# A pad of 64 bytes under the two parts of the gate and up weights

## The chip, the cores and the metric

The kernel runs on one core of a Trainium2 chip. Its metric is the device time of one execution in microseconds (us), lower is better. Before the change the median of three runs is 2303.36 us (2303.14 to 2303.79).

## The reference

One block of a streaming encoder on 512 positions of width 2048, all in float32: RMSNorm, one projection `W_in`, eight heads of a gated linear recurrence (HGRN2) and eight heads of forgetting attention (FoX), the output projection with a residual, then RMSNorm, a gated feed-forward part and a last RMSNorm. The change lies in the feed-forward part:

```python
def conv_ffn(h, w_gate, w_up, conv_w, conv_b, w_down):
    a = h @ w_gate
    a_pad = jnp.pad(a, ((0, 0), (CONV_WIDTH - 1, 0), (0, 0)))
    a = sum(conv_w[j] * a_pad[:, j:j + L] for j in range(CONV_WIDTH)) + conv_b
    return (jax.nn.silu(a) * (h @ w_up)) @ w_down
```

`w_gate` and `w_up` are 2048 x 5632, `w_down` is 5632 x 2048.

## The kernel before

Every large product is made of float32 values that are cut into two parts (hi and lo, type fp32r, one TensorE pass each), and three matmuls stand for one: hi by hi, hi by lo, lo by hi. ScalarE makes the hi part by a copy, VectorE the lo part by a subtraction.

The kernel has three stages. The first does the projections, the mixers and the output projection (lines up to 750). The second, the gate and up products, is the one that the change touches. The third does the down projection and the last norm.

The second stage goes through 44 units (`glu(f)`, lines 839 to 872), one for each 128 columns of `w_gate` and `w_up`. A unit is seven products (`product`, line 820) by Strassen's scheme on blocks of half the positions (256) and half the depth (1024). A product is eight blocks `j` of 128 columns, three matmuls each (lines 828, 829, 830), so the stage has 44 x 7 x 8 x 3 = 7392 matmuls. In each, the stationary operand is a 128 x 128 block of the weight tile `fhi` or `flo`, which TensorE loads anew for every matmul, and the moving operand is a 128 x 256 block of the activations (`b11h`, `b11l`, ... in the pools `tt` and `tl`).

The weights come from HBM into the pool `wf` (eight buffers `wq` of 4096 bytes a partition; `load`, line 769, by SyncE's queue, and with an addition on the way by GpSimd's, line 774). `prepare` (line 800) is called two products ahead (LEAD = 2): it adds where the scheme wants it (line 792), and cuts a `wq` into `fhi` (line 816, ScalarE) and `flo` (line 817, VectorE). These lie in the pool `wh`, LEAD + 2 = 4 buffers each of 4096 bytes, 32 KB a partition together. Above it lies the pool `gt` with the temporaries of a unit (`p1`, `u2`, `u3`, `a`, `uu`, `t`, `ah`, `al`); `ah` and `al` are stored to `actd` in HBM by SyncE's queue (line 872).

The order of the work is the program's: engines take their instructions in order and wait for each other by semaphores, which the framework derives from the tiles. A tile that is laid over the bytes of older, closed tiles waits for the last users of all of them. On each side of the memory pools stand one on the other, and a pool that is opened later starts where the last one ends.

Addresses: with the pads `even_sm`, `even` and `even_cm` the pools' sizes add up so that in the kernel before every tile of these pools starts at a multiple of 512 bytes within its partition: `wq` at 43520, `fhi` at 76288, `flo` at 92672, `gt` at 109056, the activations of `tl` at 27136 and of `tt` at 125440. A weight block of 128 float32 columns is 512 bytes, so each block of `fhi` and `flo` starts at such a multiple too. Tiles of the small pools don't: `onesd` (stationary operand of line 473) starts 96 bytes past a multiple of 512, `R2` (line 860) 160 bytes, `sq` (line 237) 416 bytes, and the gate weights `wf` of line 576 are blocks of 40 columns, 160 bytes each, which start 0, 160, 320, 480, 128, 288, 448 and 96 bytes past one.

Of the kernel before, what the change touches and what calls it, by code (L numbers as in the profile page):

```python
# [8 lines left out]
F32 = mybir.dt.float32  # L9
# [6 lines left out]
P = 128  # L16
# [23 lines left out]
FORM = KP * P  # L40
LEAD = 2
DMA_SUMS = True
EVEN = 376
EVEN_CM = 24
EVEN_SM = 40
# [11 lines left out]
def tile_hymba_block(ctx: ExitStack, tc: tile.TileContext, xT, wst, wgu, wdn, wfb, consts, out, out_t):  # L57
# [5 lines left out]
    def opened(name, bufs, side="left", **kw):  # L63
        cm = tc.tile_pool(name=name, bufs=bufs, side=side, reuse_waits="tile", **kw)
        pools[name] = (cm, cm.__enter__())
        return pools[name][1]

    def closed(*names):
        for name in names:
            pools.pop(name)[0].__exit__(None, None, None)  # L70
# [12 lines left out]
    even = opened("even", 1, "right")  # L83
    even.tile([P, EVEN], F32, name="even")
    cm = opened("cm", 1, "right")
# [606 lines left out]
    tt = opened("tt", 1, "right")  # L692
# [55 lines left out]
    tl = opened("tl", 1)  # L748
# [10 lines left out]


    wf = opened("wf", 8)
    wh = opened("wh", LEAD + 2)
    gt = opened("gt", 1)
    ORDER = ("a11", "s2", "a12", "s3", "s1", "a22", "s4")
# [5 lines left out]
    def load(f, name, q, q2=None):  # L770
        t = raw[f, name] = W()
        nc.sync.dma_start(out=t, in_=wgu[f, q])
        if q2 is not None:
            gp.dma_start(out=t, in_=wgu[f, q2], accum_op=ALU.add)  # L774

    def loads(f):

        if DMA_SUMS:
            load(f, "s1", 0, 1)
# [10 lines left out]
    def add(f, name, x, y, into=None):  # L790
        t = raw[f, name] = W() if into is None else into
        v.tensor_tensor(t, raw[f, x], raw[f, y], op=ALU.add)  # L792

    def sums(f):
        if not DMA_SUMS:
            add(f, "s1", "a21", "a22")
            add(f, "s3", "a21", "a11", raw[f, "a21"])
        add(f, "s2", "s1", "a11")
# [40 lines left out]
    def glu(f):  # L839
        cw = con[:, C_CW + 3 * f:C_CW + 3 * f + 3]  # L840
        g = 7 * f
        L, H = slice(0, QH), slice(QH, T)
        x, y, z, w = half(mm), half(mx), half(mm), half(mx)
        p1, u2, u3 = (G(n, (P, QH)) for n in ("p1", "u2", "u3"))
        a, uu = G("a"), G("uu")
        product(g, x)
        s.activation(p1, x, AF.Copy)
        product(g + 1, y)
        v.tensor_tensor(u2, p1, y, op=ALU.add)
        product(g + 2, x, first=False)  # L850
        s.activation(a[:, L], x, AF.Copy)
        product(g + 3, y, first=False)
        v.tensor_tensor(u3, p1, y, op=ALU.add)
        product(g + 4, z)
        v.tensor_tensor(uu[:, H], u3, z, op=ALU.add)
        product(g + 5, w)
        v.tensor_tensor(uu[:, L], u3, w, op=ALU.subtract)
        product(g + 6, z, first=False)
        v.tensor_tensor(a[:, H], u2, z, op=ALU.add)
        v.tensor_tensor(a, a, R2, op=ALU.mult)  # L860
        t = G("t")
        s.activation(t, a, AF.Identity, scale=cw[:, 2:3], bias=con[:, C_CB + f:C_CB + f + 1])
        v.scalar_tensor_tensor(t[:, 1:T], a[:, 0:T - 1], cw[:, 1:2], t[:, 1:T], op0=ALU.mult, op1=ALU.add)
        v.scalar_tensor_tensor(t[:, 2:T], a[:, 0:T - 2], cw[:, 0:1], t[:, 2:T], op0=ALU.mult, op1=ALU.add)
        v.tensor_tensor(uu, uu, nR2, op=ALU.mult)
        s.activation(t, t, AF.Silu)
        v.tensor_tensor(uu, uu, t, op=ALU.mult)
        hi, lo = G("ah", dt=F32R), G("al", dt=F32R)
        s.activation(hi, uu, AF.Copy)
        v.tensor_tensor(lo, uu, f32(hi), op=ALU.subtract)  # L870
        for i, part in enumerate((hi, lo)):
            nc.sync.dma_start(out=actd[f, i], in_=f32(part))
# [3 lines left out]
        prepare(g)  # L876
    for f in range(NF):
        glu(f)
    closed("gt", "wh", "wf", "tl", "tt")


    wr = opened("wr", 3)
# [189 lines left out]
```

## Time and profile before

| | us |
|---|---|
| median of the three runs | 2303.36 |
| the profiled execution | 2302.61 |
| its span, first to last instruction | 2300.9 |
| TensorE busy (matmul) | 2271.3 (99%) |
| VectorE busy | 1464.3 (64%) |
| ScalarE busy | 939.5 (41%) |
| granted TensorE clock, mean share | 0.995 |

The span is what the views divide; 1.7 us of the execution lie around it. A matmul's busy time holds its way through the array, so that neighbours overlap: what a stream of matmuls costs is read from the distance of their starts, not from the mean duration.

### The profile page before, as it was taken

What the parts mean: (1) busy time and instruction counts of PE and PEld (TensorE: products, weight loads), DVE (VectorE), ACT (ScalarE), POOL (GpSimd) and SP (SyncE); (2) the same over time, 40 slices, a digit from 0 to 9 for tenths busy, and PEclk for the clock granted to TensorE, in tenths of its full rate; (3) what the DMA queues carried; (4) which work ended last, traced back from release to release, by engine and by line L of the source; (5) the groups of instructions that cost most, each with busy time, mean ns of one, the idle gap of its engine ahead of it and who ended that gap; (6) DMA issues with size and microseconds to landing.
All of it is one profiled execution on the core that took longest, in us unless ns stands there. A gap on an engine that the chain in (4) does not pass through costs nothing. (4 is left out here: it accounts for less than half of the span.)

```text
span 2300.9 us, 34411 instructions
## 1 busy us (share of the span) xinstructions
PE 2271.3 (99%) x13662; PEld 2023.0 (88%) x13662; DVE 1464.3 (64%) x2194; ACT 939.5 (41%) x1484; POOL 172.0 (7%) x259
## 2 busy tenths in 40 slices
PE   8999999999999998999999999999999999999998
PEld 7888888788888887999999999999999788888886
DVE  6666467656457565888888888888888433333345
ACT  5333233334335444544444444444454222222234
POOL 4000000000000000000000000000000422000000
PEclk9999999999999999999999999999999999999999
DMA  5222222222222445877777778777776865323223
GB/s 176 84 83 83 96 77 93 75 87 76 90 83 74 142 161 170 227 205 216 209 207 211 200 207 219 213 207 209 212 197 171 316 261 194 101 96 101 92 95 116
DMA packets 112210, 352.67 MB, mean 153 GB/s; under 512 B 12816, under 2 KB 19088, under 8 KB 112048
## 3 DMA queue, kind: packets, MB, share of 16 engines
q1 hardware_dynamic: 89568, 272.67, 35.7%
q0 software_dynamic: 22336, 77.67, 15.2%
q8 instruction: 107, 1.75, 0.3%
q14 instruction: 55, 0.45, 0.1%
q10 hardware_dynamic: 144, 0.12, 0.0%
HBM read 318.96 MB, written 31.46 MB: 152 GB/s over the span
## 5 line engine op out<-in xcount | busy, mean ns | idle before, releaser
L159 DVE TENSOR_TENSOR wlo<-raw,whi 128x512 fp32r<-128x512 f32 x453 | 315.1, 697 | 456.3 <-ACT whi L158 415.9
L158 ACT ACTIVATE whi<-raw 128x512 fp32r<-128x512 f32 x453 | 285.0, 630 | 675.5 <-PE mxt L211 309.0
L816 ACT ACTIVATE fhi<-wq 128x1024 fp32r<-128x1024 f32 x308 | 326.4, 1060 | 375.9 <-PE pq L829 335.5
L817 DVE TENSOR_TENSOR flo<-wq,fhi 128x1024 fp32r<-128x1024 f32 x308 | 376.1, 1221 | 62.0 <-ACT fhi L816 59.0
L210 PE MATMUL mmt<-at,whi 128*128 128x512 f32 x896 | 354.8, 396 | 0.0
L212 PE MATMUL mmt<-at,wlo 128*128 128x512 f32 x896 | 349.7, 390 | 0.0
L211 PE MATMUL mmt<-at,whi 128*128 128x512 f32 x896 | 349.3, 390 | 0.0
L210 PE MATMUL mxt<-ot,whi 128*128 128x512 f32 x660 | 258.2, 393 | 3.5 <-ACT whi L158 2.7
L212 PE MATMUL mxt<-ot,wlo 128*128 128x512 f32 x660 | 257.4, 390 | 0.9 <-DVE wlo L159 0.9
L211 PE MATMUL mxt<-ot,whi 128*128 128x512 f32 x660 | 257.4, 390 | 0.3 <-DMA ot<-actd 0.3
L212 PEld LDWEIGHTS mmt<-at,wlo 128*128 128x128 f32 x896 | 168.2, 188 | 36.0
L210 PEld LDWEIGHTS mmt<-at,whi 128*128 128x128 f32 x896 | 168.3, 188 | 34.8 <-issue 2.0
L211 PEld LDWEIGHTS mmt<-at,whi 128*128 128x128 f32 x896 | 168.4, 188 | 33.1
L210 PEld LDWEIGHTS mxt<-ot,whi 128*128 128x128 f32 x660 | 124.2, 188 | 31.7 <-DMA ot<-actd 3.0
L211 PEld LDWEIGHTS mxt<-ot,whi 128*128 128x128 f32 x660 | 124.2, 188 | 27.4 <-DMA ot<-actd 1.6
L212 PEld LDWEIGHTS mxt<-ot,wlo 128*128 128x128 f32 x660 | 124.2, 188 | 26.7 <-DVE wlo L159 1.2
L774 POOL DMA_DIRECT2D wq<-wgu x88 | 75.9, 862 | 794.4 <-DVE flo L817 416.7
L792 DVE TENSOR_TENSOR wq<-wq 128x1024 f32<-128x1024 f32 x88 | 107.5, 1222 | 4.2 <-DMA wq<-wgu 2.7
L295 PE MATMUL mmt<-wlo,at 128*128 128x512 f32 x256 | 100.6, 394 | 4.9 <-DVE wlo L159 4.9
L828 PE MATMUL pq<-b11h,fhi 128*128 128x256 f32 x352 | 100.7, 286 | 3.6 <-ACT fhi L816 3.6
L293 PE MATMUL mmt<-whi,at 128*128 128x512 f32 x256 | 101.7, 397 | 1.6 <-ACT whi L158 1.6
L830 PE MATMUL pq<-b11h,flo 128*128 128x256 f32 x352 | 100.7, 286 | 1.3 <-DVE flo L817 1.3
(303 smaller groups left out, 5109.4 us busy)
## 6 DMA issues: line engine op xcount, KB each, us to landing
wq<-wgu SPq DMA_DIRECT2D x220, 512.0 KB, 4.5
raw<-wst SPq DMA_DIRECT2D x143, 512.0 KB, 3.4
wq<-wgu POOLq DMA_DIRECT2D x88, 512.0 KB, 7.5
raw<-wdn SPq DMA_DIRECT2D x87, 512.0 KB, 3.5
ot<-actd POOLq DMA_DIRECT2D x88, 256.0 KB, 6.2
actd<-ah SPq DMA_DIRECT2D x44, 256.0 KB, 3.4
actd<-al SPq DMA_DIRECT2D x44, 256.0 KB, 2.9
xt<-xT SPq DMA_DIRECT2D x16, 256.0 KB, 5.8
```

Of the source, the lines that this page charges most:

```text
L158: s.activation(hi, src, AF.Copy)
L159: v.tensor_tensor(lo, src, f32(hi), op=ALU.subtract)
L210: pe.matmul(ps, lhsT=a, rhs=xh[:, ts], start=(first and i == 0), stop=False)
L211: pe.matmul(ps, lhsT=a, rhs=xl[:, ts], start=False, stop=False)
L212: pe.matmul(ps, lhsT=b, rhs=xh[:, ts], start=False, stop=(last and i == n - 1))
L293: pe.matmul(pss[i], lhsT=xh[:, ts], rhs=hi, start=(k == 0), stop=False)
L295: pe.matmul(pss[i], lhsT=xh[:, ts], rhs=lo, start=False, stop=(k == KT - 1))
L792: v.tensor_tensor(t, raw[f, x], raw[f, y], op=ALU.add)
L816: s.activation(hi, t, AF.Copy)
L817: v.tensor_tensor(lo, t, f32(hi), op=ALU.subtract)
L828: pe.matmul(ps, lhsT=a, rhs=th, start=(first and j == 0), stop=False, **kw)
L830: pe.matmul(ps, lhsT=b, rhs=th, start=False, stop=(j == KP - 1), **kw)
```

## The change

A pool `sh` of one tile of 16 float32 (64 bytes a partition) is opened between `wf` and `wh`, and closed with them. Nothing writes or reads its tile. All of `wh` and `gt` lie 64 bytes higher: `fhi` starts at 76352, `flo` at 92736, `gt` at 109120. `wf`, `tl` and `tt` stay where they are, and so do all tiles of the first and the third stage.

```diff
+SHIFT = 16
...
     wf = opened("wf", 8)
+
+    sh = opened("sh", 1)
+    sh.tile([P, SHIFT], F32, name="shift")
     wh = opened("wh", LEAD + 2)
     gt = opened("gt", 1)
...
-    closed("gt", "wh", "wf", "tl", "tt")
+    closed("gt", "wh", "sh", "wf", "tl", "tt")
```

## Rows read from the trace of the kernel before

**Rows 1.** The page: span, and busy time of each engine (share, instructions).
```profile
span 2300.9 us, 34411 instructions
PE 2271.3 (99%) x13662; PEld 2023.0 (88%) x13662; DVE 1464.3 (64%) x2194; ACT 939.5 (41%) x1484; POOL 172.0 (7%) x259
```

**Rows 2.** Busy time by engine in two windows, all and middle of the second stage.
```profile
core 0: us, PE busy (x) PEld busy (x) DVE busy (x) ACT busy (x) POOL busy (x), PEclk, DMA share, GB/s
905.50:1799.00 893.50, 891.09 (x7394) 889.71 (x7394) 732.21 (x885) 436.15 (x527) 75.65 (x89) 1.00 0.77 207
920.00:1790.00 870.00, 870.00 (x7252) 870.00 (x7251) 719.98 (x863) 429.95 (x519) 72.96 (x85) 1.00 0.77 207
```

**Rows 3.** Line 830 alone: durations in ns (min/median/max), first and last start.
```profile
L830 PEld LDWEIGHTS pq<-b21h,flo x352: 192/192/192, 917.6 to 1787.0; 128*128 128x128 f32 x176
L830 PE MATMUL pq<-b21h,flo x352: 283/283/283, 917.8 to 1787.1; 128*128 128x256 f32 x176
L830 PE MATMUL pq<-n4h,flo x352: 283/283/283, 926.4 to 1795.8; 128*128 128x256 f32 x176
```

**Rows 4.** Timeline, second stage, TensorE: start, us, engine, line, op, out<-in, form.
```profile
1300.07 0.28 PE L830 MATMUL pq<-n2h,flo 128*128 128x256 f32 x1
1300.19 0.28 PE L828 MATMUL pq<-n2h,fhi 128*128 128x256 f32 x1
...
1301.99 0.28 PE L828 MATMUL pq<-b21h,fhi 128*128 128x256 f32 x1
```

**Rows 5.** Timeline, first stage, TensorE: an undisturbed stretch of 512 columns.
```profile
60.67 0.39 PE L211 MATMUL mmt<-at,whi 128*128 128x512 f32 x1
...
61.80 0.39 PE L210 MATMUL mmt<-at,whi 128*128 128x512 f32 x1
```

**Rows 6.** Line 473 alone: its loads and matmuls in ns.
```profile
L473 PEld LDWEIGHTS mxt<-ot,onesd x16: 187/188/188, 100.8 to 420.3; 128*128 128x128 f32 x16
L473 PE MATMUL mxt<-ot,onesd x16: 390/392/395, 101.0 to 420.6; 128*128 128x512 f32 x16
```

**Rows 7.** Timeline around the first use of line 473.
```profile
98.82 0.69 DVE L225 TENSOR_TENSOR ot<-ot 128x512 fp32r<-128x512 f32 x1
...
99.87 0.39 PE L211 MATMUL mmt<-at,whi 128*128 128x512 f32 x1
...
100.77 0.39 PE L212 MATMUL mmt<-at,wlo 128*128 128x512 f32 x1
101.00 0.62 PE L473 MATMUL mxt<-ot,onesd 128*128 128x512 f32 x2
101.46 0.40 PE L210 MATMUL mmt<-at,whi 128*128 128x512 f32 x1
...
103.31 0.39 PE L212 MATMUL mmt<-at,wlo 128*128 128x512 f32 x1
```

**Rows 8.** Timeline, the 32 matmuls of line 576 and the one behind them.
```profile
409.54 7.56 PE L576 MATMUL mmt<-at,ot 128*40 128x512 f32 x32
416.94 0.39 PE L293 MATMUL mmt<-whi,at 128*128 128x512 f32 x1
```

**Rows 9.** Timeline, float32 matmuls of line 463 with their own weight loads.
```profile
95.31 0.60 PE L463 MATMUL mxt<-ot,xt 128*128 128x128 f32 x4
95.75 0.39 PE L465 MATMUL mxt<-ot 128*128 128x128 f32 x2
```

**Rows 10.** Single lines of ScalarE and VectorE, ns (min/median/max).
```profile
L816 ACT ACTIVATE fhi<-wq x308: 1040/1060/1067, 904.5 to 1787.3; 128x1024 fp32r<-128x1024 f32 x154
L817 DVE TENSOR_TENSOR flo<-wq,fhi x308: 1215/1224/1228, 906.3 to 1788.4; 128x1024 fp32r<-128x1024 f32 x154
L860 DVE TENSOR_TENSOR a<-a,R x44: 691/691/694, 932.6 to 1799.5; 128x512 f32<-128x512 f32 x44
L865 DVE TENSOR_TENSOR uu<-uu,nR x44: 691/691/692, 929.7 to 1796.6; 128x512 f32<-128x512 f32 x44
L237 ACT ACTIVATE sq<-xt x15: 612/617/632, 8.2 to 39.5; 128x512 f32<-128x512 f32 x15
L869 ACT ACTIVATE ah<-uu x44: 615/615/630, 939.1 to 1804.5; 128x512 fp32r<-128x512 f32 x44
```

**Rows 11.** The stores of `al`: time to landing of its 44 transfers.
```profile
L872 SPq DMA_DIRECT2D actd<-al x44: 320/327/414, 941.0 to 1805.8; - x44
DMA to landing us min/median/max: 2.0/2.9/8.4
```

**Rows 12.** Timeline, both ends of the second stage; in brackets idle time and releaser.
```profile
904.15 0.40 ACT L702 ACTIVATE t3h<-tq 128x256 fp32r<-128x256 f32 x1
904.45 1.04 ACT L816 ACTIVATE fhi<-wq 128x1024 fp32r<-128x1024 f32 x1
905.54 0.58 PE L828 MATMUL pq<-b11h,fhi 128*128 128x256 f32 x1 [3.62 <-ACT fhi L816]
...
1798.89 3.19 POOL L895 DMA_DIRECT2D ot<-actd  x6 [16.92 <-PE pq L830]
```

## The prediction

> **What bounds the kernel.** I read the page first: TensorE is busy for 2271.3 of 2300.9 us, every other engine for 64% or less [rows 1]. Then the windows, for the stage that the change touches: it runs from 905.5 to 1799 us, and in its middle 870 us TensorE has no idle time at all, at a granted clock of 1.00, while VectorE works 719.98 us (83%) and ScalarE 429.95 (49%) [rows 2]. So this stage costs what its stream of matmuls costs, and the reader has to look at the distance between their starts. The timeline gives it: from 1300.07 to 1301.99 there are 16 steps, 1.92 / 16 = 120 ns each [rows 4]. That the step is the same all the way is seen in line 830, one of the three lines: 352 matmuls last 283 ns from minimum to maximum, and their loads 192 [rows 3]. 7392 matmuls at 120 ns are 887.0 us of the stage's 893.5; the rest, 6.5 us, is its start, where the first matmul waits for the first weight part.
>
> Of the 120 ns, 256 columns at the full clock of 2.4 GHz take 106.7. The other 13.3 ns stand beside every matmul: at 512 columns five steps take 61.80 - 60.67 = 1.13 us, 226 ns each [rows 5], which is 213.3 plus 13. It is a fixed amount, and the whole question is whether it depends on where the weight block lies.
>
> **The change part by part.** No instruction on an engine is added: the tile `shift` is never used. What moves is the address of the weight parts, from a multiple of 512 bytes to 64 bytes past it, and of a unit's temporaries.
>
> *TensorE reads `fhi` and `flo` 64 bytes higher.* 7392 loads of weights are touched, so each nanosecond in the step is 7.4 us, and one period of the 2.4 GHz clock (0.42 ns) is 3.1 us. No fp32r matmul with a full block of weights at 64 past a multiple of 512 stands in the trace; I bound it by the nearest ones.
> - Line 473 loads `onesd`, 96 past a multiple. Its 16 loads last 187 to 188 ns and its matmuls 390 to 395 [rows 6]; the aligned ones around it last 0.39 to 0.40 us. But a small disturbance starts with it: the four steps before go at 226 ns (99.87 to 100.77), and the eleven from 100.77 to 103.31 take 2.54 us, 231 each [rows 7]. That is 4.3 ns a step more. Charged wholly to the two misplaced loads, it is 11 x 4.3 / 2 = 23.5 ns a load, the upper end: 7392 x 23.5 = 174 us.
> - Line 576 loads blocks that start at eight different places, four of them multiples of 32 but not of 64, three of them (128, 320, 448) multiples of 64 off 512, one on it. All 32 steps together take 416.94 - 409.54 = 7.40 us, 231 ns each [rows 8]. That is again the slower of the two paces, 4.3 ns over the undisturbed one, but as its blocks have 40 columns and change place every second matmul, the row doesn't say whether place or shape does it.
> - Downward, no more than the 13.3 ns can go: 98.6 us. The nearest row of a matmul with its own load of 128 columns that runs closer is line 463: four in 0.44 us, 110 ns each, in plain float32 [rows 9].
>
> I take zero. Of line 473's eleven slow steps nine load aligned weights, so the slower pace isn't a price of the misplaced load itself. And its operand came late: VectorE finished the lo part at 98.82 + 0.69 = 99.51 us, 1.5 us before the matmul, so TensorE's queue will have run down and been filled again, which explains a pace that stays for ten steps and then goes. In the second stage parts are cut two products ahead. The strongest reason is the constancy itself: ScalarE, VectorE and the DMA (busy share 0.77, 207 GB/s [rows 2]) write and read the same memory at all phases while the 352 matmuls of each operand don't vary by a nanosecond [rows 3]; and the step doesn't know which of the eight blocks of 512 bytes is read. Nothing in it looks like a collision that an address could make or mend. Both ends, +174 and -98.6, are kept for the range.
>
> The Trainium skill's page "TensorE: Matmul & The Clock Gate", section "Back-to-back issue gap", gives N / 2.4 + 2.5 ns for a warm matmul that stands alone, 109.2 ns here. The trace disagrees: 120. If the difference of 10.8 ns were two reads that get in each other's way, and the pad ended it, the sum would be 80 us lower; against this, the page "SBUF — State Buffer", section "Who interferes with whom", gives TensorE two read ports, one for either operand, and by that nothing changes.
>
> *ScalarE writes `fhi`, VectorE reads it and writes `flo`, 64 bytes higher.* 308 of each, 1060 and 1224 ns. Operands off a multiple of 512 stand in the trace: line 860 reads `R2` 160 past one and takes 691 ns, line 865 with all operands on one also 691; ScalarE writes `sq` at 416 past one in 617 ns, `ah` on one in 615 [rows 10]. So the price is 0 to 2 ns of 616, at most 0.3%, up to 4 ns for each 1060 or 1224. TensorE hides it: a unit has 56 x 3 = 168 matmuls, 20.16 us, of which VectorE works 83%. If that cover were gone, 308 x 4 ns would be 1.2 us. Below zero nothing is to be had, as neither bounds the stage.
>
> *The temporaries and the stores.* `ah` and `al` are read by the DMA 64 bytes past. The 88 stores land within 2.0 to 8.4 us [rows 11], and those that the third stage reads first were issued some 840 us before. Even a doubled transfer has its cover; without it, the last pair would hold back nothing but its own late load. Zero on either side.
>
> *Waits at both ends.* A tile of `wh` now lies over one more old tile, and `fhi`'s first use waits for one more operand of the last matmuls of stage one: three matmuls, 0.7 us at most. It is covered: the first `fhi` starts at 904.45 behind ScalarE's own work that was issued at 904.15, long after these matmuls; ScalarE's order sets the start [rows 12]. At the other end GpSimd's load of the activations waits for the last matmul of the stage, 16.92 us [rows 12], and that address (the top of memory) isn't moved. Zero to +0.7 us; I take zero.
>
> The sum: 2302.61 us for the profiled execution (span 2300.9 and 1.7 around it) plus 0. Against the median of the runs the profiled execution is 0.75 us short, so I forecast the median, 2303.4 us.
>
> **The rivals.**
> - *Slower: a block that doesn't start on a multiple of 512 costs the slower pace.* Place: each of the 7392 loads in lines 828 to 830. Price: the 4.3 ns between the two paces. For it: line 473 is where a misplaced full block first comes into an undisturbed stream, and the slower pace starts exactly there, at the step before its matmul [rows 7]; line 576 keeps it for all its 32 steps [rows 8]. Against: the aligned steps behind line 473 are slow as well, and the late operand explains them. It gives 7392 x 4.3 = 31.8 us, 2335 us. It decides from 0.62 ns a step on, as that is 4.6 us. By the upper end it would be 2477 us.
> - *Faster: part of the 13.3 ns is two reads that begin at the same place within 512 bytes, and the pad parts them.* For it: in this stage every load and every moving operand start on a multiple of 512, and a float32 matmul with a load runs at 110 ns [rows 9]. Against: line 576 with its eight places never comes below the undisturbed pace on average [rows 8], and line 473 doesn't either. To 110 ns it gives 7392 x 10 = 73.9 us, 2229 us; a smaller step lies between: one period of 1.2 GHz, 0.83 ns, gives 6.2 us, 2297 us. By the page's 109.2 it would be 2223.
> - *The pad doesn't move what it should, or moves more.* The allocation is in steps of 32 bytes, so 64 bytes do move the pool; and since nothing above `gt` stands on this side, no other stage sees it. This is inside the forecast.
>
> **How the numbers follow.** About 0.2% (4.6 us) is what a measurement of this kernel can tell from no change. No change: 0.57. Slower: 0.25, most of it at the 32 us of the first rival, a fifth of it beyond. Faster: 0.18, spread from 2229 to 2298 us. The forecast's own range is 2302 to 2305 us. The range up to 2336 takes in four fifths of the slower case (0.20), and down to 2296 a quarter of the faster one (0.05): 0.57 + 0.20 + 0.05 = 0.82.
>
> **What would show it.** In the changed kernel the same 16 steps in the middle of the stage should take 1.92 us, line 830 stay at 283/283/283 and its loads at 192, and the stage last 893.5 us. Each is read alone: a matmul pace off 120 ns by the same amount everywhere would prove a rival on the operand's place, upward or downward; a VectorE or ScalarE duration off 1224 or 1060 ns with the pace kept would be a price that is hidden. A stage that keeps its pace and still grows would say that a wait at its ends was overlooked. I am wrong if the step changes by more than half a nanosecond.

## The result, and the profile after

The changed kernel takes 2253.39 us (median of four runs), the kernel before 2303.57: the ratio is 0.978, with a 95% interval of 0.977 to 0.980. It is faster by 50 us, and the forecast of no change was wrong. One of the four runs took 2285.87 us and is left out of the ratio; one of six runs of a kernel below took 2286.64 us, and no profile shows what happened in either.

The page of the changed kernel, to be held against [rows 1], gives its span and the busy times. The line numbers of the second stage are four higher than before.

```profile
span 2250.8 us, 34411 instructions
PE 2224.2 (99%) x13662; PEld 1976.2 (88%) x13662; DVE 1457.9 (65%) x2194; ACT 940.1 (42%) x1484; POOL 172.6 (8%) x259
```

The instructions are the same in number, and TensorE is busy for the same share of the span: the work itself got shorter. The windows of the second stage (as in [rows 2]: length, busy time and count of TensorE, of its weight loads, of VectorE, ScalarE and GpSimd, then clock and DMA) show no idle time of TensorE in the middle of the stage, and the same clock:

```profile
905.00:1752.00 847.00, 842.51 (x7395) 840.94 (x7394) 726.44 (x885) 439.30 (x530) 78.35 (x94) 1.00 0.82 219
920.00:1740.00 820.00, 820.00 (x7237) 820.00 (x7237) 711.39 (x862) 430.85 (x518) 72.96 (x85) 1.00 0.82 219
```

The timeline of TensorE in the middle of the stage, against [rows 4]:

```profile
1299.95 0.28 PE L832 MATMUL pq<-t3h,fhi 128*128 128x256 f32 x1
1300.07 0.28 PE L833 MATMUL pq<-t3l,fhi 128*128 128x256 f32 x1
...
1301.99 0.28 PE L832 MATMUL pq<-t3h,fhi 128*128 128x256 f32 x1
```

From the first to the last of these lie 18 steps, 2.04 us: 113.3 ns each instead of 120. Line 834 (830 before, [rows 3]) says that it is so from 916 to 1737 us: 352 matmuls, minimum, median and maximum the same.

```profile
L834 PEld LDWEIGHTS pq<-b21h,flo x352: 187/188/188, 916.2 to 1737.3; 128*128 128x128 f32 x176
L834 PE MATMUL pq<-b21h,flo x352: 276/276/276, 916.3 to 1737.4; 128*128 128x256 f32 x176
```

The two ends of the stage, and the lines of ScalarE and VectorE that make the parts (minimum, median and maximum in ns), answer to [rows 10, 12]:

```profile
903.14 1.04 ACT L820 ACTIVATE fhi<-wq 128x1024 fp32r<-128x1024 f32 x1
904.23 0.58 PE L832 MATMUL pq<-b11h,fhi 128*128 128x256 f32 x1 [3.63 <-ACT fhi L820]
...
1748.54 3.19 POOL L899 DMA_DIRECT2D ot<-actd  x6 [15.82 <-PE pq L834]
...
L820 ACT ACTIVATE fhi<-wq x308: 1040/1066/1072, 903.1 to 1737.6; 128x1024 fp32r<-128x1024 f32 x154
L821 DVE TENSOR_TENSOR flo<-wq,fhi x308: 1215/1219/1227, 905.0 to 1738.7; 128x1024 fp32r<-128x1024 f32 x154
```

So the books close. From the first matmul of the stage to the loads that its last one releases it was 1798.89 - 905.54 = 893.35 us and is 1748.54 - 904.23 = 844.31: 49.04 less, and 7392 x 6.67 ns are 49.3. Ahead of the stage 1.31 us are gained, behind it 0.25 lost; that is scatter, as the kernels below, whose first stage differs at most in addresses, start the second between 904.2 and 905.7 us. Together 50.1, the difference of the spans. What makes the parts is 6 ns slower on ScalarE and 5 faster on VectorE, and hidden: TensorE doesn't wait for it in the middle of the stage.

### The profile page after: what moved, and what is told of

Read it like the earlier page. It is cut to its first block, busy times and chain, and to the rows that moved or that the text cites. A ratio compares the mean times of both kernels' runs of the same rounds, so it can differ in the third digit from the quotient of the medians.

```text
span 2250.8 us, 34411 instructions
## 1 busy us (share of the span) xinstructions
PE 2224.2 (99%) x13662; PEld 1976.2 (88%) x13662; DVE 1457.9 (65%) x2194; ACT 940.1 (42%) x1484; POOL 172.6 (8%) x259
## 5 line engine op out<-in xcount | busy, mean ns | idle before, releaser
L294 PE MATMUL mmt<-whi,at 128*128 128x512 f32 x256 | 101.6, 397 | 0.9 <-ACT whi L159 0.9
L295 PE MATMUL mmt<-whi,at 128*128 128x512 f32 x256 | 100.7, 393 | 0.0
```

The source lines that it names most:

```text
L294: pe.matmul(pss[i], lhsT=xh[:, ts], rhs=hi, start=(k == 0), stop=False)
L295: pe.matmul(pss[i], lhsT=xl[:, ts], rhs=hi, start=False, stop=False)
```

## The experiments

Three theories stood after the result. The first: what counts is where the stationary block lies against the moving operand. The second: the place of the stationary block alone. The third: not TensorE's reads, but the temporaries and who writes and reads them. A kernel below ran once where no number of runs is given, and what is concluded from it goes by the steps in its trace.

**The temporaries alone.** The pad goes above the weight parts, so that only `gt` moves.

```diff
     wf = opened("wf", 8)

+    wh = opened("wh", LEAD + 2)
     sh = opened("sh", 1)
     sh.tile([P, SHIFT], F32, name="shift")
-    wh = opened("wh", LEAD + 2)
     gt = opened("gt", 1)
...
-    closed("gt", "wh", "sh", "wf", "tl", "tt")
+    closed("gt", "sh", "wh", "wf", "tl", "tt")
```

> The pad of 64 bytes lies above the weight parts, so only the unit's temporaries (gt) move. Theory 1 (where TensorE's weight block lies against its moving operand sets the 13.3 ns beside each matmul) and theory 2 (the place of the weight block alone sets it): the step stays 120 ns, 2303 us. Theory 3 (it is the temporaries, read and written by ScalarE, VectorE and the store): the step falls to 113.3 ns, 2253 us.

Measured 2303.4 us (before, beside it, 2301.81). Line 834 of this kernel has the old duration:

```profile
L834 PE MATMUL pq<-b21h,flo x352: 283/283/283, 917.3 to 1786.7; 128*128 128x256 f32 x176
```

The third theory falls.

**The moving operand alone.** In the kernel before, 64 bytes are taken from one pad of the right side and given to another, so that `tt` and `pq` move up by 64 and nothing else that TensorE reads in the two later stages.

```diff
-EVEN = 376
-EVEN_CM = 24
+EVEN = 360
+EVEN_CM = 40
```

> No pad under the weight parts. Instead the activations move up 64 bytes: the moving operands of blocks 0 to 6 of the second stage (pool tt) and of the third stage (pool pq); block 7 (pool tl) stays. Theory 1 (relative place): blocks 0 to 6 leave 120 ns, to 113.3 if the sign of the distance doesn't matter; block 7 stays at 120; the third stage leaves 226.7 too, to 220; 7392 x 7/8 x 6.7 = 43 us and about 2100 x 6.7 = 14 us less, 2246 us. Theory 2 (place of the weight block alone): 120 and 226.7 everywhere, 2303 us.

Measured 2296.75 us (before, beside it, 2301.81; expected 2246). Blocks 1 to 6 of one product, the timeline of TensorE:

```profile
1249.94 0.28 PE L828 MATMUL pq<-b11h,fhi 128*128 128x256 f32 x1
...
1252.06 0.29 PE L828 MATMUL pq<-b11h,fhi 128*128 128x256 f32 x1
```

18 steps in 2.12 us are 117.8 ns. The weight parts lie where they always lay, and the step has changed: the second theory falls as well. But the sign of the distance matters (it isn't 113.3). Block 7, which stayed where it was, didn't stay at 120: its three steps take 123.3 on average. And the third stage became slower, not faster. There the same stretch of 300 us holds fewer matmuls, here first the kernel before, then this one:

```profile
1850.00:2150.00 300.00, 300.00 (x1325) 248.43 (x1324) 101.97 (x150) 69.53 (x110) 22.58 (x43) 1.00 0.39 139
```
```profile
1850.00:2150.00 300.00, 300.00 (x1312) 246.16 (x1311) 101.80 (x150) 68.89 (x109) 17.10 (x33) 1.00 0.37 128
```

**Both moved.** The same edit on the changed kernel: weight parts and moving operands 64 bytes up.

> Both at once: weight parts and the activations of blocks 0 to 6 are 64 bytes up, block 7's activations are not. Theory 1 (relative place): blocks 0 to 6 are back at 120 ns and block 7 is at 113.3; the third stage as in the run that moves the activations alone; about 2303 - 6 - 14 = 2283 us. Theory 2 (weight block alone): 113.3 in all eight blocks, 2253 us, third stage unchanged.

Measured 2303.14 us (expected 2283). Blocks 3 to 6 of one product:

```profile
1254.65 0.28 PE L832 MATMUL pq<-b11h,fhi 128*128 128x256 f32 x1
...
1256.09 0.29 PE L832 MATMUL pq<-b11h,fhi 128*128 128x256 f32 x1
```

12 steps in 1.44 us: 120.0 again, with the weights at the place that gave 113.3 before. That is the relative place. It also rules out that the gain came from how ScalarE and VectorE write and read the weight parts, as these lie here where they lie in the changed kernel. Block 7, whose moving operand stays, didn't reach 113.3 as expected: it and the three blocks behind it go at changing steps (112 to 122 ns, averaged over many products). Here the pace needs some ten steps to settle after a change of place. And the third stage took back what the second won.

**A scan by units.** `wh` has tiles of 4096 + 512 bytes, and each unit takes its own slice of them. A smaller pad `EVEN` makes room; by it the activations of blocks 0 to 6 move up by 1024 bytes, four times 256.

```diff
-EVEN = 376
+EVEN = 120
...
+    PLACES = [16 * f for f in range(32)] + [4, 8, 12, 20, 24, 28, 36, 40, 56, 60, 68, 0]
+
+    def part(name, f):
+        off = PLACES[f] // 4
+        return wh.tile([P, FORM + 128], F32R, name=name, tag=name)[:, off:off + FORM]
...
-        hi = wh.tile([P, FORM], F32R, name="fhi", tag="fhi")
-        lo = wh.tile([P, FORM], F32R, name="flo", tag="flo")
+        hi, lo = part("fhi", f), part("flo", f)
```

> Each unit f has its own place for its weight parts: 16 f bytes past a multiple of 512 for units 0 to 31, then 4, 8, 12, 20, 24, 28, 36, 40, 56, 60, 68 and 0. The step of each unit is read from the trace. If the cost falls steadily with the distance, 64 (113.3 ns) lies halfway and 128 gives 106.7; if 64 merely parts two halves of 128 bytes, the step is 113.3 at odd multiples of 64 and 120 at even ones; if only being off the multiple of 512 counts, all but 0 give 113.3. Both theories on the weight block expect a curve; theory 3 expects 120 throughout.

Measured 2289.45 us. The first matmuls of neighbouring units, each 168 steps apart: places 64, 192, 256 and 320.

```profile
990.60 0.28 PE L832 MATMUL pq<-b11h,fhi 128*128 128x256 f32 x1
1009.65 0.28 PE L832 MATMUL pq<-b11h,fhi 128*128 128x256 f32 x1
...
1149.49 0.28 PE L832 MATMUL pq<-b11h,fhi 128*128 128x256 f32 x1
1169.28 0.28 PE L832 MATMUL pq<-b11h,fhi 128*128 128x256 f32 x1
...
1228.63 0.28 PE L832 MATMUL pq<-b11h,fhi 128*128 128x256 f32 x1
1248.79 0.28 PE L832 MATMUL pq<-b11h,fhi 128*128 128x256 f32 x1
...
1308.34 0.28 PE L832 MATMUL pq<-b11h,fhi 128*128 128x256 f32 x1
1327.38 0.28 PE L832 MATMUL pq<-b11h,fhi 128*128 128x256 f32 x1
```

19.05, 19.79, 20.16 and 19.04 us: 113.4, 117.8, 120.0 and 113.3 ns. All sixteen places from 256 on give the step of the place 256 lower, within 0.1 ns: place 256 is like 0, place 320 like 64. And 192 is what the moved activations showed (64 bytes up for one operand is 64 down, so 192, for the other). None of the simple curves that were expected holds.

**The fine curve.** The same in steps of 4 bytes, four products a place, and in the third stage (512 columns) in steps of 8 bytes, five pieces a place. The weight tiles of the third stage get 256 bytes more for it, so that they start by turns on a multiple of 512 and 256 past one; the places of this stage count from there.

```diff
...
+    PLACES = [4 * p for p in range(64)] + [320, 320, 64, 64, 328, 392, 464, 476, 264, 72, 480, 256, 0]
...
+        off = PLACES[g // 4] // 4
...
+    ws.places = [8 * (p // 5 % 32) for p in range(NPIECE_D)]
```

> The relative place held in the runs before; this one draws its curve. Second stage: the weight parts of four products at a time lie 4 p bytes past a multiple of 512, p = 0 to 63, and a dozen places beyond 256 that repeat earlier ones. Third stage (512 columns): its weight parts lie 8 q bytes past, q = 0 to 31, five pieces each. If it is the relative place within 256 bytes (theory 1 as the scan of units left it), places beyond 256 give the step of the place 256 lower, 64 stays the lowest near 113.3, and the third stage has a curve of its own around 226.7 with its lowest place at 64 too, near 220. If instead the place of single units mattered by chance (what ran beside them), repeated places differ.

Measured 2300.4 us. Three products (72 steps) each at the places 52, 56 and 108, and then 48 steps of the third stage each at the places 64 and 120:

```profile
1063.57 0.28 PE L835 MATMUL pq<-n1h,fhi 128*128 128x256 f32 x1
1071.73 0.28 PE L835 MATMUL pq<-b11h,fhi 128*128 128x256 f32 x1
1074.56 0.28 PE L835 MATMUL pq<-n2h,fhi 128*128 128x256 f32 x1
1083.04 0.29 PE L835 MATMUL pq<-n1h,fhi 128*128 128x256 f32 x1
...
1221.36 0.28 PE L835 MATMUL pq<-n1h,fhi 128*128 128x256 f32 x1
1230.16 0.28 PE L835 MATMUL pq<-b11h,fhi 128*128 128x256 f32 x1
...
1909.58 0.40 PE L213 MATMUL mxt<-ot,whi 128*128 128x512 f32 x1
1920.78 0.39 PE L213 MATMUL mxt<-ot,whi 128*128 128x512 f32 x1
...
2007.46 0.39 PE L213 MATMUL mxt<-ot,whi 128*128 128x512 f32 x1
2018.35 0.40 PE L213 MATMUL mxt<-ot,whi 128*128 128x512 f32 x1
```

8.16, 8.48 and 8.80 us are 113.3, 117.8 and 122.2 ns; 11.20 and 10.89 us are 233.3 and 226.9. Worked out in the same way from the starts, the steps in ns at some places (bytes):

```
place                0     8    24    52    56    64    68    76    80    88    96   108   128   192   224
256 columns        120   115.6 121.8 113.4 117.8 113.4 118.4 113.4 118.8 113.4 118.7 122.2 118.6 117.8 116.6
512 columns        226.7 230.7 230.0  -    233.4 233.3  -     -    232.0 233.3 234.2  -    232.5 228.9 233.3
```

The lowest step at 256 columns is 113.3, at four places (52, 64, 76 and 88), and 4 bytes beside them it is 118 to 120. All repeated places of this kernel agree (320 with 64, 264 with 8, 480 with 224). For 512 columns nearly the whole curve lies above what the multiple of 512 already gives; the expectation of 220 at 64 failed.

The two scans put the weight parts at the same addresses, so their common places can be held together. At two of them the paces differ: 144, and 240 as well. The first two lines are the scan by units at place 144, 144 steps apart; the other two the fine curve at the same place, 72 steps apart.

```profile
1092.46 0.28 PE L832 MATMUL pq<-n2h,fhi 128*128 128x256 f32 x1
1109.50 0.28 PE L832 MATMUL pq<-b11h,fhi 128*128 128x256 f32 x1
...
1324.14 0.28 PE L835 MATMUL pq<-n4h,fhi 128*128 128x256 f32 x1
1332.78 0.28 PE L835 MATMUL pq<-n2h,fhi 128*128 128x256 f32 x1
```

17.04 us are 118.3 ns a step, 8.64 us are 120.0, and neither changes while the place lasts; at 240 it is 120.0 against 117.3. So at some places the stream can settle at more than one pace. What decides it isn't shown; the scans come to a place from different neighbours (from 128 and from 140 in this case). Place 64, where all loads of a stretch have it, gave 113.3 or 113.4 in every kernel.

**The hi parts alone.** `fhi` at place 64, `flo` at 0.

```diff
...
+    PLACES = [64] * 44
...
+        off = PLACES[f] // 4 if name == "fhi" else 0
```

> Only the hi parts lie 64 bytes past, the lo parts on the multiple of 512. If each load pays by its own place, two of three steps are 113.3 and one 120: 115.6 on average, 7392 x 4.4 = 33 us less than before, 2270 us. If the stream locks into a pattern that needs all loads at the same place, the step is 117 or more, at least 2281 us.

Measured 2285.93 us, a pace of 117.8 ns in every unit. Line 834:

```profile
L834 PE MATMUL pq<-b21h,flo x352: 281/281/281, 917.4 to 1770.7; 128*128 128x256 f32 x176
```

The loads don't pay one by one (that would be 115.6 on average); the stream settles in a pattern that all of them make. The duration of a line is as steady as in the other kernels, though the three steps of a block are not quite alike: 118.3, 117.5 and 117.5 ns on average.

**Place 76, and the odd places of the third stage.** The kernel of the fine curve with other numbers.

```diff
...
+    PLACES = [76] * 77
...
+    ws.places = [8 * (p // 5 % 32) + 4 for p in range(NPIECE_D)]
```

> Second stage: all weight parts 76 bytes past a multiple of 512, one of the four places of the fine curve with 113.3 ns (52, 64, 76, 88). If the place alone sets the step, all 44 units run at 113.3. Third stage (512 columns): the places left out before, odd multiples of 4 bytes, five pieces each. If 512 columns have better places as well, some run below 226.7, at 220; if the multiple of 512 is already the best place for 512 columns, none does, and the mean is near 232.

Measured 2264.41 us. All units at place 76 go at 113.3 ns, as line 837 (834 of the changed kernel) shows:

```profile
L837 PE MATMUL pq<-b21h,flo x352: 276/276/276, 917.6 to 1738.7; 128*128 128x256 f32 x176
```

Of the 32 new places for 512 columns two, 132 and 156, come to 226.8, the others lie between 230 and 238. So the third stage has nothing to win by its place, and 113.3 ns is the lowest that the scans found for the second with one place for all loads.

**The third stage at 64 as well.**

```diff
...
+    PLACES = [64] * 77
...
+    ws.places = [64] * NPIECE_D
```

> The pad of 64 bytes in both stages: second stage as in the changed kernel (113.3 ns, 50 us less than before), and the weight parts of the third stage 64 bytes past too. By the fine curve 512 columns run at 233.3 ns there against 226.7: 1980 steps x 6.6 = 13 us lost, 2303 - 50 + 13 = 2266 us. If what a place is worth were the same for all widths, the third stage would win 13 us: 2240 us.

Measured 2265.18 us (four runs; 0.984 of before, 0.982 to 0.985). The third stage, TensorE:

```profile
1950.03 0.39 PE L213 MATMUL mxt<-ot,whi 128*128 128x512 f32 x1
...
1959.83 0.39 PE L213 MATMUL mxt<-ot,whi 128*128 128x512 f32 x1
```

42 steps in 9.80 us, 233.3 ns: the place that wins 6.7 ns a step at 256 columns loses 6.7 at 512.

**Other sizes of the pad.** The change itself with `SHIFT = 80` (320 bytes) and `SHIFT = 64` (256 bytes).

> The pad of the change made 320 bytes (64 + 256). If the relative place counts within 256 bytes, the step is 113.3 ns and the time that of the change, 2253 us. If the distance itself counts, it may be anything between 2253 and 2303 us.

> The pad made 256 bytes. By the period of 256 bytes the step is 120 ns again and the time 2303 us, although the weight parts are moved four times as far as by the change. If leaving the multiple of 512 counts, the step falls below 120 ns.

Measured 2253.34 us (median of six; interval of the ratio 0.977 to 0.985) and 2303.12 us (ten runs; ratio 1.000, 0.999 to 1.001). Line 834 of the one and of the other:

```profile
L834 PE MATMUL pq<-b21h,flo x352: 276/276/276, 916.9 to 1738.0; 128*128 128x256 f32 x176
```
```profile
L834 PE MATMUL pq<-b21h,flo x352: 283/283/283, 916.7 to 1786.1; 128*128 128x256 f32 x176
```

A pad of 256 bytes does nothing, one of 64 + 256 does what 64 does.

**Line 473 put right.** This tests the step of the prediction by which the trace of before was read. In the kernel before, `onesd` is allocated ahead of the pad in its pool, so that it lies on a multiple of 512; all else stays.

```diff
-    cm.tile([P, EVEN_CM], F32, name="even_cm")
...
     onesd = cm.tile([P, P], F32R, name="onesd")
+    cm.tile([P, EVEN_CM], F32, name="even_cm")
```

> The kernel before with one tile moved: onesd, the stationary operand of line 473, lies on a multiple of 512 bytes instead of 96 past one; its operand still comes as late as before. If the slower pace of eleven steps that begins at line 473 is the price of its place, it is gone: 226.7 ns through line 473 in all eight heads, 8 x 11 x 4.3 ns = 0.4 us less. If it comes from the late operand, as the prediction had it, the eleven steps stay at 231 ns.

Measured 2301.41 us (before, beside it, 2302.34). The same stretch as [rows 7], VectorE's row and TensorE's:

```profile
98.07 0.69 DVE L225 TENSOR_TENSOR ot<-ot 128x512 fp32r<-128x512 f32 x1
...
99.57 0.39 PE L210 MATMUL mmt<-at,whi 128*128 128x512 f32 x1
...
100.02 0.39 PE L212 MATMUL mmt<-at,wlo 128*128 128x512 f32 x1
100.25 0.61 PE L473 MATMUL mxt<-ot,onesd 128*128 128x512 f32 x2
100.70 0.39 PE L210 MATMUL mmt<-at,whi 128*128 128x512 f32 x1
...
102.51 0.39 PE L212 MATMUL mmt<-at,wlo 128*128 128x512 f32 x1
```

The operand comes as late as before (98.76, 1.5 us ahead of the matmul), and the eleven steps from 100.02 to 102.51 take 2.49 us, 226.4 each: the slower pace is gone here, and so in seven of the eight heads. There it was the place. In one head it stays, though no operand lies off a multiple of 512:

```profile
214.25 0.50 PE L293 MATMUL mmt<-whi,at 128*128 128x512 f32 x1
214.58 0.39 PE L294 MATMUL mmt<-whi,at 128*128 128x512 f32 x1
...
215.74 0.39 PE L293 MATMUL mmt<-whi,at 128*128 128x512 f32 x1
```

The stream was interrupted ahead of line 473 (steps of 0.30 and 0.33 us, the second from 214.25 to 214.58), and the five steps behind it, to 215.74, take 232 ns each before it is back at 226.7. So an interrupted stream needs some steps too; in the other seven heads it wasn't interrupted.

## Why the prediction was wrong

The step that failed is the first of the part by part: "I take zero" for 7392 loads that move by 64 bytes. It measured -6.67 ns a step and 49 us, within its own lower bound of -98.6. Its reasons, one by one:

- *That line 473's slower pace is no price of the misplaced load, as most of the slow steps load aligned weights, and that the late operand explains it.* False for the seven heads in which the stream runs on: with the same lateness and another place it is gone. An interruption does leave slow steps, as the remaining head shows; but in the seven the operand was ready 1.5 us before its matmul, and up to line 473 the stream kept its steps of 226 to 227 ns. A place can disturb the pace for about ten steps behind it, as the activations moved with the weights showed too (block 7 and the blocks behind it). The rows of before did carry the effect, and I argued it away.
- *That the constancy speaks against an effect of the address.* False: the stream locks into a pattern that repeats, and three arrangements with three paces are each constant in their durations: 283, 281 and 276 ns from minimum to maximum.
- *That the step doesn't know which of the eight blocks is read.* True and worthless: the blocks are 512 bytes apart, two whole periods of 256.

One reading of the trace of before was wrong too, without weight for the result. The 6.5 us that the stage lasts beyond its steps are not the wait for the first weight part, which lies ahead of 905.54 us [rows 12]. Behind that wait of 3.62 us the stage starts at a granted clock of 0.50 (1.2 GHz), and some twenty steps take 213 ns, with waits for later parts between them; the changed kernel starts its stage in the same way.

```profile
905.50:910.00 4.50, 3.19 (x13) 2.90 (x14) 1.98 (x5) 0.00 (x0) 0.87 (x1) 0.50 1.03 291
```

The slower rival had the effect right and its sign wrong for this width. At 512 columns, from which its rows came, leaving the multiple of 512 does cost at most places (226.7 to 233.3 at 64 and 234.2 at line 473's 96, shown in the third stage); at 256 columns the same place gains. The price was carried from one width to another without a row that allowed it.

The faster rival, at 0.18, had the direction right, and that the place of one read against the other matters. That the pad helps by parting them is not shown: at place 108 they are parted too, and the step is 122.2. Its price of 10 ns a step was one and a half times the measured 6.67, and the 110 ns it came from belong to matmuls of 128 columns in plain float32 [rows 9], which say nothing of 256 columns of fp32r. Of the 13.3 ns beside each matmul the pad takes half. By the Trainium skill's page "TensorE: Matmul & The Clock Gate", section "Back-to-back issue gap", the gap of a warm matmul that stands alone would be 109.2 ns, an estimate from its N / 2.4 + 2.5; this stream doesn't reach it, the trace says 113.3 at the best place of all. The Trainium skill's page "SBUF — State Buffer", section "Who interferes with whom", gives TensorE a port for each operand and calls the two independent; the measurement differs in so far as moving either operand alone changes the pace (120 to 113.3 and to 117.8 ns), and it decides.

The other terms held: ScalarE and VectorE within 6 ns of their durations (the prediction allowed 4) and hidden, and nothing beyond scatter ahead of the stage and behind it, so no cost of waits at the ends or of the stores.

Shown is that moving TensorE's two operands against each other changes the pace, that the change repeats after 256 bytes, and that it depends on the width of the moving operand. The place doesn't always settle the pace alone (144 and 240). Why a place gives one pace and not another is not shown: no run tells how the two reads meet.

No run points to a version clearly below the changed kernel: its place is one of the four lowest for the second stage, and the third stage already has the lowest for its width. What is left is line 473, by its steps some 0.3 us. Other pairs of places for the hi and the lo parts than the one tried were not scanned.

## What to carry to other kernels

Where a stream of matmuls runs without gaps and its step is a fixed amount over its columns, the place of the weight block against the moving operand is worth a scan: let each unit of a loop take its own offset within a wider tile, and read the step of each from one profile. Then measure the chosen place in a kernel of its own, since a place can show another pace in another order of places. A price measured at one width of the moving operand is not carried to another. A duration that never varies is no sign that the address doesn't matter.

## What the runs showed of the hardware

- At 256 columns the settled step of a fp32r matmul with its own load of 128 columns lies between 113.3 and 122.2 ns as its operands move against each other; at 512 columns between 226.7 and 238.
- The curve repeats after 256 bytes (a pad of 256 bytes leaves 120 ns, one of 320 gives 113.3 like one of 64), and its best places are narrow: 113.4 at 52 and at 64, 117.8 at 56.
- At two of the places that both scans have, 144 and 240, the same addresses settled at two paces: 118.3 and 120.0, 120.0 and 117.3 ns.
- Some ten steps behind a change of place or a misplaced load go at another pace: eleven from line 473 on, nine behind block 7. Five steps of 232 ns followed an interruption.
- Four of the paces, 113.3 and 120 ns at 256 columns, 226.7 and 233.3 at 512, are 106.7 plus 6.7 or 13.3 ns, and 213.3 plus 13.3 or 20 ns (106.7 and 213.3 are the columns at 2.4 GHz).
- A weight load lasts 192 ns in the trace at the pace of 120, 188 at 113.3.
